# Second heads' keys and values three ticks later, a wider spread of the last convolution taps, and closer LayerNorm steps in a hybrid transformer block

## The chip, the core and the metric

The program runs on one core of one Trainium2 chip. The metric is the device time of one execution in microseconds (us), the median over several executions. The core has five engines that matter here, each of which works through its own instructions strictly in program order: PE (TensorE, matmuls and transposes; its weight loads are shown as PEld), DVE (VectorE), ACT (ScalarE), POOL (GpSimd) and SP, which here does nothing but issue DMAs. Engines meet through semaphores only.

## The reference, cut to what matters

One decoder layer on 512 tokens of width 2048, all in float32:

```python
h = rms_norm(x); proj = h @ w_in
out_a = dilated_mixture(aq, ak, av)          # 8 heads x 64, three (window, dilation) pairs
out_b = silu(layer_norm(causal_depthwise_conv31(bu * sigmoid(bg)) + conv_b))   # 512 channels
out_c = band_attention(cq, ck, cv, 127, sinks)   # 16 query heads, 2 key/value heads x 64
x = x + concat(out_a, out_b, out_c) @ w_out
h2 = rms_norm(x)
x = x + (silu(h2 @ w_gate) * (h2 @ w_up)) @ w_down    # width 5632
```

Queries and keys of both attentions are RMS-normalised per head first.

## The kernel before

Activations lie transposed, channels on the 128 partitions and the 512 tokens along the free axis. Each float32 factor is split in two parts of a reduced float type: a "high" part, cast by ACT, and a "low" part, the rest, subtracted by DVE (for the `mix` rows of attention C by POOL). A product is then three matmuls of 128x512: high x high, high x low and low x high (`mm3`, lines 325 to 327).

**The stages.** (1) The input projection, 30 column tiles of 128 (`PROJ`): four at once at the start, then 26 by `project`. (2) The output projection: 16 row tiles of `mix` (`ROWS`: c0 c3 c1 c5 c2 c7 c4 c6, then a0 a1 b2 b1 b0 b3 a2 a3) times 16 output tiles, in two halves: `half == 0` uses the eight c rows, `half == 1` the eight a and b rows. (3) The feed-forward part, with a seven-product scheme for its matrix products. It takes the last two thirds of the time and is not touched.

**The order of the work** is written by hand. `Ticks` is a list of functions with due times. The matmul loops call `ticks.tick()` at fixed places, and a tick emits everything that is due into the queues of the engines, in the order in which it was registered:

- `project` ticks once for two k steps, that is, every 6 matmuls, 8 ticks for a tile. The 26 tiles take ticks 0 to 207, so that tile number p of `PROJ` (from 0) is done at tick 8 x (p - 3).
- `first_two` (two output tiles together, 6 matmuls for each row) ticks after every row: 208 to 215 in half 0.
- The other 14 output tiles of half 0 tick after every 12 matmuls, twice for a tile: 216 to 243. Then comes half 1.

So attention heads, convolution and LayerNorm of earlier tiles run on DVE, ACT and POOL beside the projection matmuls, with their own few PE instructions (score matmuls, transposes, `weigh`) put between them.

**What touches the change.**

- Keys: `do_k` normalises a key tile (two heads), `twin` copies each head's half to the other half of the partitions with two DMAs on SP, `high` (L708 to L711) casts both heads on ACT and one tick later `low` (L713 to L715) subtracts both on DVE. Values of attention A: `load_v` fetches a tile from DRAM, `high` (L730 to L733) casts both heads and `low` (L735 to L737) subtracts them. Head 1 of a tile of A starts its scores 7 ticks after head 0 (`A_TICKS`), head 1 of C 12 ticks after head 0.
- Convolution: 4 channel tiles x 31 taps, each one DVE instruction (`tap`, L541), spread over the ticks. With n the tap's number, tap n >= 93 (the fourth tile) comes at tick 154, 156, 158, 160, 162, 163 and so on to 203, then a pause of 9 ticks, then 214, 216 and 217.
- LayerNorm over the 512 channels: `ln_sum` (three adds on DVE, then the split of the sum), `ln_mean` (a memset on DVE and two matmuls), `ln_center` (four DVE subtractions), `ln_square` (four squares on ACT, three adds on DVE), `ln_var` (`token_scale`: four PE transposes, a DVE reduction, a DVE scale and a power on POOL), `ln_out` (`all_rows`: a transpose on PE, a copy on ACT, a DMA to DRAM, `put`, and a DMA back that spreads the row over the partitions, `back`), `ln_scale` (four POOL products and four silu on ACT), and then `split_mix` of the rows b2, b1, b0, b3. They are at ticks 219, 221, 222, 225, 228, 231, 232 (put), 233 (back), 235 (scale) and 236 to 239 (splits).
- In `first_two` and after it, `split_rows(k)` emits the split of row k + 2 when row k is about to be multiplied. The low part of a c row is `ml_c`, on POOL (L1067).
- `residual` (L1168) adds an output tile to x on DVE. From the third output tile on, the accumulators are in two PSUM banks by turns (`column`), so a tile can begin when the add of the tile before the last is done.
- `next_unit` splits the weights two uses ahead (L283 on ACT, L284 on DVE) and issues weight loads (L271) on SP as buffers come free.

Of the kernel before, what the change touches and what calls it, by code (L numbers as in the profile page):

```python
# [9 lines left out]
F32 = mybir.dt.float32  # L10
F32R = mybir.dt.float32r
# [4 lines left out]
P = 128  # L16
T = 512
NT = T // P
# [10 lines left out]
TAPS = 31  # L29
NB = 4  # L30

OUT_ORDER = (list(range(16)), [n + o for n in range(6) for o in (0, 8)] + [6, 7, 14, 15])
TAPS_FROM, TAPS_FAST, TAP_TICKS = 19, 47, 1.8
TAPS_2 = 6
V_AHEAD = 2
WARM = 8
PAUSE_FROM, TAP_PAUSE = 205, 9


SQ, KW, VD, TD, EV = 3, 4, 4, 2, 1  # L40
# [2 lines left out]
ROW_KEYS = ("ck", "ak2")  # L43
FOLD_AT = (2, 4, 3)
FOLDED = 2 + sum(FOLD_AT) + 2
ROWS_FROM, ROWS_AT, LN_ROWS_AT = 2, (1, 2, 3), (1, 1, 2)


C_TICKS = (1, 6, 2, 2, 2, 2, 4, 1, 5)
# [86 lines left out]
def kernel(ctx: ExitStack, tc: tile.TileContext, xT, wi, wo, wgu, wd, cst_in, outT):  # L136
    nc = tc.nc
# [18 lines left out]
    ticks = Ticks()  # L156

    def slot(name, dt=F32, cols=T):
        return sp.tile([P, cols], dt, name=name, tag="s")
# [4 lines left out]
    def bank(name, cols=T):  # L164
        return psum["banks"].tile([P, cols], F32, name=name, tag="b")

    def column(name):
        return psum["tiles"].tile([P, T], F32, name=name, tag="c")
# [287 lines left out]
    for k in range(KT):  # L456
# [11 lines left out]
        hi, lo = h_hl.pop(k)  # L468
        h_hi.append(hi)
        h_lo.append(lo)  # L470
        for i in range(NT):
            s = slice(i * P, (i + 1) * P)
# [11 lines left out]
    def project(name):  # L484
        b = column(name)
        for half in range(2):
            wh, wl = next_unit(split=split_in_steps)
            for kk in range(8):
                k = 8 * half + kk
                s = slice(kk * P, (kk + 1) * P)  # L490
                mm3(b, wh[:, s], wl[:, s], h_hi[k], h_lo[k], k == 0, k == KT - 1)
                if kk % 2 == 1:
                    ticks.tick()
        return b

    def all_rows(out, src, heads, name, waits, then, *args):

        n = NT * heads
        b = bank(name + "t")
        nc.tensor.transpose(b[:n, :P], src, ident)  # L500
        rows = cp.tile([2 * NT, P], F32, name=name + "w", tag="rows", bufs=2)
        nc.scalar.copy(rows[:n], b[:n, :P])
        d = tc.dram_tile([n, P], F32, name=name)

        def put():
            nc.sync.dma_start(d, rows[:n])
            ticks.after(waits[1], back)

        def back():
            for h in range(heads):  # L510
                part = out if heads == 1 else out[HALF[h]]
                nc.sync.dma_start(part.rearrange("p (i c) -> p i c", i=NT),
                                  bass.AP(tensor=d.tensor, offset=d.offset + h * P,
                                          ap=[[0, P // heads], [heads * P, NT], [1, P]]))
            ticks.after(waits[2], then, *args)
        ticks.after(waits[0], put)
# [5 lines left out]
    hconv, yconv = {}, {}  # L522
# [22 lines left out]

    ln = {}

    def ln_sum():
        s = slot("lns")
        nc.vector.tensor_add(s, yconv[0], yconv[1])  # L550
        nc.vector.tensor_add(s, s, yconv[2])
        nc.vector.tensor_add(s, s, yconv[3])
        ln["hi"], ln["lo"] = slot("lnh", F32R), slot("lnl", F32R)
        nc.scalar.copy(ln["hi"], s)
        nc.vector.tensor_sub(ln["lo"], s, ln["hi"].bitcast(F32))
# [112 lines left out]
    def do_k(box, b, name, gi):  # L668
        def then(r):
            if name in ROW_KEYS:  # L670
                ticks.after(ROWS_FROM, rows_of, r)
            else:
                ticks.after(KW, widen, r)

        raw, at_r = head_scales(b, name, name == "ak2", then)
        box["k at"] = at_r + (ROWS_FROM + sum(ROWS_AT) - 2 if name in ROW_KEYS else KW) + TD + 7
        both = []

        def rows_of(r):
            wide = slot(name + "wide")  # L680
            all_rows(wide, r.rearrange("p a b -> p (a b)"), 2, name + "d", ROWS_AT, scale, wide)

        def widen(r):
            wide = slot(name + "wide")
            nc.scalar.copy(wide.rearrange("p (a b c) -> p a b c", a=NT, b=2),
                           r[:, :, :, None].to_broadcast([P, NT, 2, HD]))
            ticks.after(1, flip, wide)

        def flip(wide):
            b2 = bank(name + "t")  # L690
            for i in range(NT):
                nc.tensor.transpose(b2[:, i * P:(i + 1) * P], wide[:, i * P:(i + 1) * P], ident)
            ticks.after(1, scale, b2)

        def scale(b2):
            for h in range(2):
                both.append(slot(f"{name}{h}"))
                nc.vector.scalar_tensor_tensor(both[h][HALF[h]], raw[HALF[h]], gqk[HALF[h], gi:gi + 1], b2[HALF[h]],
                                               op0=ALU.mult, op1=ALU.mult)
            ticks.after(1, twin)  # L700

        def twin():
            for h in range(2):
                nc.sync.dma_start(both[h][HALF[1 - h]], both[h][HALF[h]])
            ticks.after(TD, high)

        def high():
            box["k"] = [(slot(f"{name}h{h}", F32R), slot(f"{name}l{h}", F32R)) for h in range(2)]  # L708
            for h in range(2):
                nc.scalar.copy(box["k"][h][0], both[h])  # L710
            ticks.after(1, low)  # L711

        def low():  # L713
            for h, (hi, lo) in enumerate(box["k"]):
                nc.vector.tensor_sub(lo, both[h], hi.bitcast(F32))  # L715
            if gi == 1:
                box["k0"] = [slot(f"{name}0{h}", F32R, 2 * P) for h in range(2)]
                for k0, src in zip(box["k0"], both):
                    nc.scalar.copy(k0[:, :P], src[:, :P])
                    nc.vector.tensor_sub(k0[:, P:], src[:, :P], k0[:, :P].bitcast(F32))  # L720

    def load_v(box, j):
        name = f"av{j}"
        t = slot(name + "s")
        nc.sync.dma_start(t.rearrange("p (i c) -> p i c", i=NT),
                          bass.AP(tensor=vd.tensor, offset=vd.offset + j * P, ap=[[T, P], [P * T, NT], [1, P]]))
        src = t.rearrange("p (a b c) -> p a b c", a=NT, b=2)

        def high():
            box["v"] = [slot(f"{name}{h}", F32R).rearrange("p (a b c) -> p a b c", a=NT, b=2) for h in range(2)]  # L730
            for h in range(2):
                nc.scalar.copy(box["v"][h][:, :, h], src[:, :, h])
            ticks.after(1, low)  # L733

        def low():  # L735
            for h, v in enumerate(box["v"]):
                nc.vector.tensor_sub(v[:, :, 1 - h], src[:, :, h], v[:, :, h].bitcast(F32))  # L737

        box["v at"] = ticks.now + V_AHEAD + 2
        ticks.after(V_AHEAD, high)  # L740

    def do_v(box, b, name):
        vs = slot(name + "s")
# [315 lines left out]
    mix, late = {}, []  # L1059
# [20 lines left out]
    g4 = b = None  # L1080
    taps = [(j, i) for j in range(NB) for i in range(TAPS)]
    for n, (j, i) in enumerate(taps):
        at_tap = TAPS_FROM + min(n, TAPS_FAST) + int(max(n - TAPS_FAST, 0) * TAP_TICKS) + TAPS_2 * (j >= 2)
        at_tap += TAP_PAUSE * (at_tap >= PAUSE_FROM)
        ticks.after(at_tap, tap, j, i)
    t_ln = at_tap + 2
    ticks.after(t_ln, ln_sum)
    ticks.after(t_ln + 2, ln_mean)
    ticks.after(t_ln + 3, ln_center)
    ticks.after(t_ln + 6, ln_square)  # L1090
    ticks.after(t_ln + 9, ln_var)
    ticks.after(t_ln + 12, ln_out, mix)

    shared = {}
    boxes, waiting = {}, []
    for name in PROJ[HEAD4:]:
        kind, what, j = name[0], name[1], name[2:]
# [3 lines left out]
        b = project(name)  # L1101
# [3 lines left out]
        if kind == "c":  # L1105
            box = Heads(shared) if j else shared
        else:
            box = boxes.setdefault(j, {})
# [15 lines left out]
    b = box = boxes = shared = waiting = None  # L1124
# [123 lines left out]
    for half in range(2):  # L1248
        for i, n in enumerate(OUT_ORDER[half]):
# [4 lines left out]
            if half == 1 and i == 2:  # L1254
                split_up_to(at["use"] + 1)
                ticks.drain()
                b = None
                open_banks(banks=4 - COLUMN_BANKS, high=2)
            b = column(f"o{half}_{n}")
            wh, wl = next_unit()  # L1260
            for kk in range(8):
                k = 8 * half + kk
# [4 lines left out]
                s = slice(kk * P, (kk + 1) * P)  # L1267
# [387 lines left out]
    for g in range(G_STEPS + N_DOWN):  # L1655
# [6 lines left out]
        for i, q in enumerate(ORDER):  # L1662
# [37 lines left out]
            n = LOADS + (t >= -2)  # L1700
# [3 lines left out]
            if N_TURNED - 2 <= t < N_TURNED:  # L1704
                n = 4 - (t % 2 == 0)
# [91 lines left out]
```

## Time and profile before

| what | us |
|---|---|
| median of 3 runs (lowest, highest) | 1850.84 (1850.51, 1851.1) |
| the profiled execution | 1851.08 |
| its span, first to last instruction | 1849.3 |
| PE busy in the span | 1841.7 |
| DVE, ACT, POOL busy | 1528.4, 1368.8, 1098.3 |

The profiled execution lies 0.24 us above the median and 1.8 us above its own span. Times of the trace are us from the start of the span. An instruction is shown with its line, engine, operation and tile names (output<-inputs, buffer numbers left out); a bracket at its end gives the idle time of its engine just before it and what released it. PE's matmuls overlap, so that their starts, not their durations, tell the pace.

### The profile page before, as it was taken

Reading aid. Unit: us, or ns where it says so; the run is one execution under the profiler, and the core shown is the slowest. Engines: PE = TensorE matmul, PEld = TensorE weight load, DVE = VectorE, ACT = ScalarE, POOL = GpSimd, SP = SyncE. Lnnn points to the kernel's source line nnn. Section 1 sums busy time; section 2 is a strip of 40 time slices with the busy share of each in tenths; the row PEclk is TensorE's granted clock in tenths of the full one; section 3 lists DMA queues with packets and bytes.
Section 4 is the critical chain, followed back from the end, with each engine's and each line's share of the span. In section 5 each row is a group of like instructions: output and inputs, shape, how many; then the busy total and the mean of one; then the engine's idle time right before and its main releaser. Section 6 shows DMA issues by size and latency. Waiting matters only on the chain.

```text
span 1849.3 us, 26795 instructions
## 1 busy us (share of the span) xinstructions
PE 1841.7 (100%) x8509; PEld 1533.7 (83%) x8509; DVE 1528.4 (83%) x2314; ACT 1368.8 (74%) x1957; POOL 1098.3 (59%) x703
## 2 busy tenths in 40 slices
PE   9999999999999999999999999999999999999999
PEld 7888888888888888888888888888888888888888
DVE  7688799997589888898888888888888677779887
ACT  6225655554466788889989889898898987777775
POOL 5004454462252568666685666857667777766786
PEclk9999999999999999999999999999999999999999
DMA  7435343433287359788787887787879786488984
GB/s 263 136 112 168 114 149 97 114 122 128 99 295 273 126 180 293 220 261 277 230 276 229 279 266 228 264 245 264 278 240 380 222 298 222 164 284 281 302 238 125
DMA packets 326461, 404.29 MB, mean 219 GB/s; under 512 B 81816, under 2 KB 216624, under 8 KB 326320
## 3 DMA queue, kind: packets, MB, share of 16 engines
q1 hardware_dynamic: 326176, 402.57, 67.8%
q8 instruction: 68, 1.11, 0.3%
q14 instruction: 73, 0.60, 0.1%
q10 hardware_dynamic: 144, 0.01, 0.0%
HBM read 312.31 MB, written 82.59 MB: 214 GB/s over the span
## 4 chain that ended last, share of the span: by engine, by line
PE 74%; DVE 0%; issue 0%; DVEq 0%
PE out L1446 62%; PE out L1338 6%; PE o L325 2%; PE o L326 2%; PE o L327 2%; PE out L1330 0%; PE a3o L935 0%; PE a3o L934 0%; PE a3t L910 0%; PE n2s L367 0%; DVE y L1635 0%; DVEq L1635 0%
## 5 line engine op out<-in xcount | busy, mean ns | idle before, releaser
L1446 PE MATMUL out<-wh,h 128*128 128x512 f32 x2464 | 609.0, 389 | 0.1
L1446 PEld LDWEIGHTS out<-wh,h 128*128 128x128 f32 x2464 | 462.3, 188 | 96.8 <-issue 0.5
L1446 PE MATMUL out<-wl,h 128*128 128x512 f32 x1232 | 329.3, 389 | 0.0
L1446 PEld LDWEIGHTS out<-wl,h 128*128 128x128 f32 x1232 | 231.2, 188 | 48.0
L1446 PE MATMUL out<-wh,a 128*128 128x512 f32 x896 | 221.3, 389 | 0.0
L1446 PEld LDWEIGHTS out<-wh,a 128*128 128x128 f32 x896 | 168.2, 188 | 34.9
L1446 PE MATMUL out<-wl,a 128*128 128x512 f32 x448 | 119.7, 389 | 0.0
L1549 DVE TENSOR_TENSOR G<-G,out 128x512 f32<-128x512 f32 x132 | 83.9, 677 | 18.1 <-PE out L1446 18.1
L1446 PEld LDWEIGHTS out<-wl,a 128*128 128x128 f32 x448 | 84.1, 188 | 17.5
L541 DVE SCALAR_TENSOR_TENSOR y<-bu,cst,y 128x511 f32<-128x511 f32 (+14 forms) x120 | 91.1, 759 | 1.5
L283 ACT CAST wh<-w 128x1024 fp32r<-128x1024 f32 (+1 forms) x41 | 42.0, 1030 | 53.4 <-PE o L326 27.9
L1338 PE MATMUL out<-a,wh 128*128 128x512 f32 x330 | 80.1, 391 | 0.0
L303 ACT CAST wh<-w 128x1024 fp32r<-128x1024 f32 x52 | 54.6, 1050 | 33.4 <-PE bg L326 8.7
L307 DVE TENSOR_TENSOR wl<-w,wh 128x1024 fp32r<-128x1024 f32 x52 | 66.4, 1279 | 9.5 <-ACT wh L303 9.4
L1546 DVE TENSOR_TENSOR G<-G,out 128x512 f32<-128x512 f32 x110 | 68.6, 681 | 5.7 <-PE out L1446 5.7
L1338 PEld LDWEIGHTS out<-a,wh 128*128 128x128 f32 x330 | 60.2, 188 | 11.4
L1587 DVE STREAM_TRANSPOSE z<-s 128x256 f32<-128x256 f32 x88 | 60.1, 683 | 3.0
L284 DVE TENSOR_TENSOR wl<-w,wh 128x1024 fp32r<-128x1024 f32 (+1 forms) x41 | 51.7, 1262 | 8.4 <-ACT wh L283 8.0
L325 PE MATMUL o<-mh_c,wh 128*128 128x512 f32 x128 | 51.4, 401 | 1.1 <-ACT a31e L866 1.1
L327 PE MATMUL o<-mh_c,wl 128*128 128x512 f32 x128 | 50.1, 391 | 0.0
L326 PE MATMUL o<-ml_c,wh 128*128 128x512 f32 x128 | 50.1, 391 | 0.0
L1491 DVE TENSOR_TENSOR Y<-Y,out 128x512 f32<-128x512 f32 x48 | 30.8, 685 | 17.9 <-PE out L1446 17.9
(2777 smaller groups left out, 5127.0 us busy)
## 6 DMA issues: line engine op xcount, KB each, us to landing
h<-hd SPq DMA_DIRECT2D x200, 256.0 KB, 5.7
od<-a SPq DMA_DIRECT2D x154, 256.0 KB, 6.6
a<-od SPq DMA_DIRECT2D x154, 256.0 KB, 5.9
w<-in_wi SPq DMA_DIRECT2D x59, 512.0 KB, 3.6
w<-in_wo SPq DMA_DIRECT2D x32, 512.0 KB, 3.4
hd<-h SPq DMA_DIRECT2D x56, 256.0 KB, 5.5
zd<-z SPq DMA_DIRECT2D x44, 256.0 KB, 4.8
x<-in_xT SPq DMA_DIRECT2D x16, 256.0 KB, 7.0
```

The lines of the kernel that those rows point to most:

```text
L284: eng.tensor_sub(lo[:, :n], t[:, :n], hi[:, :n].bitcast(F32))
L303: nc.scalar.copy(hi, t)
L307: nc.vector.tensor_sub(lo, t, hi.bitcast(F32))
L325: nc.tensor.matmul(out, wh, xh, start=start, stop=False)
L326: nc.tensor.matmul(out, wh, xl, start=False, stop=False)
L327: nc.tensor.matmul(out, wl, xh, start=False, stop=stop)
L541: nc.vector.scalar_tensor_tensor(yconv[j][:, i:], hconv[j][:, :T - i], c, yconv[j][:, i:], op0=ALU.mult, op1=ALU.add)
L1338: nc.tensor.matmul(out, lhs[:, s], rhs, start=begin, stop=last and low == flip[0] and x is xs[-1], skip_group_check=True)
L1446: nc.tensor.matmul(to[h], x[:, h * P:(h + 1) * P], v[:, j], start=sub == 0 and h not in started, stop=sub == 1 and n in (len(todo) - 1, le ...
L1546: op(t, t, b)
L1549: nc.vector.tensor_add(t, t, b)
L1587: nc.vector.transpose(to[:, :, h], s[:, cols].rearrange("p (c b) -> p b c", b=8))
```

## The change

It has three parts.

1. Keys' and values' head 1: `high` and `low` become functions of one head. Head 0 stays where it was, head 1 comes `OTHER` = 3 ticks later, for `do_k` and for `load_v`. The copies for the first key block of attention C (`k0`) go with their head.
2. Taps: taps of the fourth tile are 2.0 ticks apart (1.8 before), and the pause from tick 205 on is 5 ticks (9 before). They come at 154, 156 and so on by twos to 204, then at 211, 213, 215, 217 and 219.
3. LayerNorm: the first two adds of the sum move from DVE to POOL and to tick 209 (`ln_sum_3`); the rest comes at 221 (sum), 222 (mean), 223 (center), 224 (square), 226 (variance), 228 (out), 229 (put), 230 (back), 231 (scale), 232 to 235 (splits).

```diff
-TAPS_FROM, TAPS_FAST, TAP_TICKS = 19, 47, 1.8
+TAPS_FROM, TAPS_FAST, TAP_TICKS, TAP_TICKS_3 = 19, 47, 1.8, 2.0
-PAUSE_FROM, TAP_PAUSE = 205, 9
+PAUSE_FROM, TAP_PAUSE = 205, 5
+OTHER = 3
-ROWS_FROM, ROWS_AT, LN_ROWS_AT = 2, (1, 2, 3), (1, 1, 2)
+ROWS_FROM, ROWS_AT, LN_ROWS_AT = 2, (1, 2, 3), (1, 1, 1)
+LN_SUM_3, LN_AT = 12, (1, 2, 3, 5, 7)
...
+    def ln_sum_3():
+        s = ln["sum"] = slot("lns")
+        nc.gpsimd.tensor_add(s, yconv[0], yconv[1])
+        nc.gpsimd.tensor_add(s, s, yconv[2])
     def ln_sum():
-        s = slot("lns")
-        nc.vector.tensor_add(s, yconv[0], yconv[1])
-        nc.vector.tensor_add(s, s, yconv[2])
+        s = ln.pop("sum")
         nc.vector.tensor_add(s, s, yconv[3])
...
-            ticks.after(TD, high)
+                ticks.after(TD + h * OTHER, high, h)
+        def high(h):
+            hi, lo = box["k"][h] = (slot(f"{name}h{h}", F32R), slot(f"{name}l{h}", F32R))
+            nc.scalar.copy(hi, both[h])
+            ticks.after(1, low, h, hi, lo)
+        def low(h, hi, lo):
+            nc.vector.tensor_sub(lo, both[h], hi.bitcast(F32))
...
-        ticks.after(V_AHEAD, high)
+        for h in range(2):
+            ticks.after(V_AHEAD + h * OTHER, high, h)
...
-        at_tap = TAPS_FROM + min(n, TAPS_FAST) + int(max(n - TAPS_FAST, 0) * TAP_TICKS) + TAPS_2 * (j >= 2)
+        slow = max(n - 3 * TAPS, 0)
+        at_tap = TAPS_FROM + min(n, TAPS_FAST) + TAPS_2 * (j >= 2)
+        at_tap += int(max(n - slow - TAPS_FAST, 0) * TAP_TICKS + slow * TAP_TICKS_3)
         at_tap += TAP_PAUSE * (at_tap >= PAUSE_FROM)
     t_ln = at_tap + 2
+    ticks.after(t_ln - LN_SUM_3, ln_sum_3)
     ticks.after(t_ln, ln_sum)
-    ticks.after(t_ln + 2, ln_mean)
-    ticks.after(t_ln + 3, ln_center)
-    ticks.after(t_ln + 6, ln_square)
-    ticks.after(t_ln + 9, ln_var)
-    ticks.after(t_ln + 12, ln_out, mix)
+    for n, fn in enumerate((ln_mean, ln_center, ln_square, ln_var)):
+        ticks.after(t_ln + LN_AT[n], fn)
+    ticks.after(t_ln + LN_AT[4], ln_out, mix)
```

More of the change, by code (lines that the diff above doesn't have):

```diff
@@ L704, in twin @@
                 nc.sync.dma_start(both[h][HALF[1 - h]], both[h][HALF[h]])
-            ticks.after(TD, high)
-        def high():
-            box["k"] = [(slot(f"{name}h{h}", F32R), slot(f"{name}l{h}", F32R)) for h in range(2)]
+            box["k"] = [None, None]
             for h in range(2):
[L710 to L715, printed above, removed]
+                ticks.after(TD + h * OTHER, high, h)
[5 more added lines that the diff above has]
+            nc.vector.tensor_sub(lo, both[h], hi.bitcast(F32))
             if gi == 1:
[L717 to L720, printed above, removed]
+                k0 = slot(f"{name}0{h}", F32R, 2 * P)
+                box.setdefault("k0", []).append(k0)
+                nc.scalar.copy(k0[:, :P], both[h][:, :P])
+                nc.vector.tensor_sub(k0[:, P:], both[h][:, :P], k0[:, :P].bitcast(F32))
     def load_v(box, j):
@@ L727, in load_v, with high, low @@
         src = t.rearrange("p (a b c) -> p a b c", a=NT, b=2)
[L729 to L737, printed above, removed]
+        def high(h):
+            box["v"][h] = slot(f"{name}{h}", F32R).rearrange("p (a b c) -> p a b c", a=NT, b=2)
+            nc.scalar.copy(box["v"][h][:, :, h], src[:, :, h])
+            ticks.after(1, low, h)
+        def low(h):
+            v = box["v"][h]
+            nc.vector.tensor_sub(v[:, :, 1 - h], src[:, :, h], v[:, :, h].bitcast(F32))
+        box["v"] = [None, None]
         box["v at"] = ticks.now + V_AHEAD + 2
-        ticks.after(V_AHEAD, high)
+        for h in range(2):
+            ticks.after(V_AHEAD + h * OTHER, high, h)
     def do_v(box, b, name):
```

## Prediction

> **What bounds the kernel now.** I read the page first for the engine that is full, then whom PE waited for, then the queues at those places.
>
> ```profile
> span 1849.3 us, 26795 instructions
> ...
> PE 1841.7 (100%) x8509; PEld 1533.7 (83%) x8509; DVE 1528.4 (83%) x2314; ACT 1368.8 (74%) x1957; POOL 1098.3 (59%) x703
> ```
>
> PE is busy for 1841.7 of 1849.3 us. The change adds and removes no PE instruction: it can win only what PE loses between its instructions, or make PE lose more. The view of PE's waits lists the losses (us in total, times, longest):
>
> ```profile
> PE idle L416 <- DVE bones L356: 1.4, 1, 1.4
> PE o L325 <- ACT a31e L866: 1.1, 1, 1.1
> PE a0o L935 <- DVE a0pl L921: 0.7, 1, 0.7
> PE c60s L821 <- ACT c40e L866: 0.6, 1, 0.6
> PE lnm L562 <- DVE a21e L873: 0.3, 1, 0.3
> ```
>
> The first is the start of the program; the other four lie in stages that the change touches. Here they are in PE's timeline (start, duration, instruction, idle before it), with a fifth place at 394 us where PE is slowed without a gap that counts as idle:
>
> ```profile
> 280.09 0.27 PE L991 MATMUL c21t<-ident,c71e 128*128 128x128 f32 x1
> 280.93 0.38 PE L821 MATMUL c60s<-ck,cq 128*128 128x256 f32 x1 [0.57 <-ACT c40e L866]
> ...
> 366.19 0.33 PE L934 MATMUL a0o<-a0ph,av 128*128 128x256 f32 x1
> 367.22 0.39 PE L935 MATMUL a0o<-a0pl,av 128*128 128x256 f32 x1 [0.70 <-DVE a0pl L921]
> ...
> 394.36 0.48 PE L325 MATMUL o<-mh_c,wh 128*128 128x512 f32 x1
> 394.86 0.50 PE L326 MATMUL o<-ml_c,wh 128*128 128x512 f32 x1
> ...
> 421.64 0.39 PE L326 MATMUL o<-ml_c,wh 128*128 128x512 f32 x1
> 421.87 0.39 PE L327 MATMUL o<-mh_c,wl 128*128 128x512 f32 x1
> 422.53 0.47 PE L562 MATMUL lnm<-lnh,part 128*128 128x512 f32 x1 [0.28 <-DVE a21e L873]
> ...
> 481.20 0.39 PE L327 MATMUL o<-mh_c,wl 128*128 128x512 f32 x1
> 482.72 0.47 PE L325 MATMUL o<-mh_c,wh 128*128 128x512 f32 x1 [1.13 <-ACT a31e L866]
> ```
>
> A 128x512 matmul follows the one before after 0.23 (421.64 to 421.87); I take half of that, 0.11, for 256 columns and for a transpose (an estimate). The losses against that pace: 280.93 - 280.09 - 0.11 = 0.73; 367.22 - 366.19 - 0.11 = 0.92; 422.53 - 421.87 - 0.23 = 0.43; 482.72 - 481.20 - 0.23 = 1.29. Together 3.37. At 394 it is 394.86 - 394.36 - 0.23 = 0.27. These are all the change can win, 3.6 us or 0.2%.
>
> **The change part by part.** DVE's timeline at the first loss, at its last idle stretch before the second, and at the second, third and fourth:
>
> ```profile
> 276.37 2.09 DVE L715 TENSOR_TENSOR ak2l<-ak,ak2h 128x512 fp32r<-128x512 f32 x2
> 279.57 0.23 DVE L856 TENSOR_SCALAR c40d<-c40d,nsink 128x4 f32<-128x4 f32 x1
> ...
> 338.82 0.57 DVE L847 CUSTOM_DVE_ANT_0 a00s<-a00s,bias_a 128x384 f32<-128x384 f32 x1 [2.46 <-PE a00s L824]
> ...
> 365.87 0.76 DVE L737 TENSOR_TENSOR av<-av2s,av 128x256 fp32r<-128x256 f32 x2
> 366.74 0.42 DVE L921 TENSOR_TENSOR a0pl<-a0t,a0ph 128x256 fp32r<-128x256 f32 x1
> 367.08 0.72 DVE L541 SCALAR_TENSOR_TENSOR y<-bu,cst,y 128x489 f32<-128x489 f32 x1
> ...
> 416.63 0.98 DVE L551 TENSOR_TENSOR lns<-lns,y 128x512 f32<-128x512 f32 x1
> 422.22 0.17 DVE L560 MEMSET part<- 128x128 f32 x1
> ...
> 474.53 0.69 DVE L1067 TENSOR_TENSOR ml_b<-y,mh_b 128x512 fp32r<-128x512 f32 x1 [4.35 <-ACT mh_b L1066]
> 481.89 0.68 DVE L1168 TENSOR_TENSOR xr<-xr,o 128x512 f32<-128x512 f32 x1
> ```
>
> *Key halves, first loss.* ak2 is done at tick 120; its low parts come at tick 145, just ahead of c40's row maxima (tick 146), whose last step (279.57) releases c40's exponentials, and those free the score bank that c60s needs (tick 148). In the new order head 1's cast comes at 147, behind those exponentials, and its subtraction at 148. One of the two ak2l, 2.09 / 2 = 1.05, leaves the queue ahead of 279.57. That covers 0.73: gain 0.73. Late next would be c60's own maxima, with 1.05 more in front, at tick 152, four ticks of at least 1.4 each (6 x 0.23) after the subtraction; I cost that at nothing, covered by those 5.5 us; without the cover it costs 1.05.
>
> *Value halves and taps, second loss.* a0pl's last part is due at tick 195. The same tick has both av2 subtractions ahead of it; head 1's moves to 198: 0.38. ak1's head 1 moves from 192 to 195, still ahead, worth nothing. Between tick 178 and tick 195 the taps are 9 instead of 10 (0.72), and DVE has no idle stretch of over 0.1 there after the 2.46 that end at 338.82. 0.38 + 0.72 = 1.10 covers 0.92: gain 0.92. The wider taps themselves return 0.72 each at ticks 211 to 219, where there are five instead of three; DVE loses 1.44 there, but `ln_sum`'s two adds are gone from it. Casts, subtractions and slots are the same in number, and no DMA moves in the first two parts: `twin` and `load_v` issue as before.
>
> *The sum's first two adds, now on POOL.* They are emitted at tick 209, that is after row 1 of `first_two` and first in that tick, so behind row 3's low part and ahead of row 4's. POOL's timeline there, its group of six such low parts (busy us, mean ns | idle before them), one of them that ran long, and the four products of `ln_scale` (min/median/max ns):
>
> ```profile
> 390.47 1.29 POOL L1067 TENSOR_TENSOR ml_c<-mix_c,mh_c 128x512 fp32r<-128x512 f32 x1
> 391.75 1.75 POOL L877 TENSOR_SCALAR a11e<-a11e,a11d 128x384 f32<-128x384 f32 x1
> 393.47 2.78 POOL L1067 TENSOR_TENSOR ml_c<-mix_c,mh_c 128x512 fp32r<-128x512 f32 x2
> 396.24 1.73 POOL L877 TENSOR_SCALAR a11e<-a11e,a11d 128x512 f32<-128x512 f32 x1
> ...
> L1067 POOL TENSOR_TENSOR ml_c<-mix_c,mh_c 128x512 fp32r<-128x512 f32 x6 | 8.9, 1489 | 0.0
> ...
> 383.97 2.26 POOL L1067 TENSOR_TENSOR ml_c<-mix_c,mh_c 128x512 fp32r<-128x512 f32 x1
> ...
> L583 POOL TENSOR_TENSOR y<-y,lrs x4: 1284/1286/1298, 467.4 to 471.1; 128x512 f32<-128x512 f32 x4
> ```
>
> Each row starts as the one before ends, and the six ml_c from 382 to 401 us had no idle time before them (0.0, the last column of their group). Row 4's low part, the first of the two at 393.47, is what the matmul at 394.86 is short of: 393.47 + 1.39 (half of 2.78) = 394.86. So what is put ahead of it goes onto PE whole. The nearest rows are other two-input 128x512 operations of POOL: 1.28 (L583), 1.49 as the mean of the six from 382 to 401 us, 2.26 at most. I take the mean of that stretch: 2 x 1.49 = 2.98 lost, between 2.57 and 4.52, and nothing if the queue has run ahead by then. Rows 5 to 7 ask for no more: PE is late by the same amount, and POOL gives one low part after the other at its pace of before.
>
> *LayerNorm, third loss.* lnm waits for the memset at 422.22, which stands in DVE's queue behind everything up to tick 220. In the new order the two adds (the second took 0.98) are gone from this queue and lnm comes at 222, in the middle of an output tile, instead of 221, at a tile's end where a `residual` add and a weight subtraction stand ahead: gain 0.43. The closer steps: center (223) needs lnm; square (224) and variance (226) are two ticks apart, at least 2 x 12 x 0.23 = 5.5, in which DVE has three adds and about 3 us of other steps; variance to out (228) has again 5.5. I cost these at nothing; the cover is two ticks of matmuls for each.
>
> *LayerNorm, fourth loss.* ACT, SP and PE here:
>
> ```profile
> 468.68 0.81 ACT L585 ACTIVATE y<-y,cst 128x512 f32<-128x512 f32 x1 [3.39 <-POOL y L583]
> ...
> 451.85 0.33 SPq L271 DMA_DIRECT2D w<-in_wo  x1
> 460.25 0.32 SPq L506 DMA_DIRECT2D lrd<-lrdw  x1
> 463.31 0.35 SPq L512 DMA_DIRECT2D lrs<-lrd  x1
> ...
> 469.65 0.48 PE L325 MATMUL o<-mh_c,wh 128*128 128x512 f32 x1
> ```
>
> The view blames the exponential a31e. By the code the tile that begins at 482.72 needs the bank of the tile before the last, whose `residual` add on DVE ran from 481.89 to 482.57; DVE had sat 4.35 until 474.53 for ACT's mh_b, and ACT stood behind the silu, which waited for POOL, that is, for the broadcast (3.39 at 468.68). Everything from out on comes 3 to 4 ticks earlier, some 10 us, so that this jam is past when the tile of 482.72 begins: gain 1.29. What is late next: the silu's products start at tick 231. `put` stands in SP's queue ahead of the weight load of 451.85, `back` behind it; with 4.1 from the issue to POOL's start (463.31 to 467.4), the row would be there at about 452.7 + 4.1 = 456.8, the silu end near 463, the weight cast at 464, the weight subtraction at 465, the `residual` add for the tile that begins at tick 235 (469.65 in PE's row) at about 469. It fits by half a us: nothing, with 0 to 4 as its bounds.
>
> **The sum.** -0.73 - 0.92 - 0.43 - 1.29 + 2.98 = -0.39 us. On the profiled 1851.08 that is 1850.69, and on the median, 0.24 lower, 1850.45.
>
> **The rivals.** *POOL hides the adds.* For it: the DVE steps that feed POOL come earlier. Against: the group's idle time of 0.0. Then 3.37 is won: 1847.5.
>
> *The adds are slow.* POOL's rows of one shape take 1.28 or 2.26; if both adds fall on the long one, 4.52 - 3.37 = +1.15: 1852.0. The Trainium skill, page "SBUF — State Buffer", section "Who interferes with whom", says that a VectorE instruction with two SBUF inputs and a GpSimd instruction that reads SBUF exclude each other, the later one waiting for the whole of the earlier. By that rule, with DVE full here, this rival is the case. The trace agrees in part: 2.26 occurs once among six.
>
> *The moved halves free nothing.* If DVE's queue is as long at 279 and 366 us as before, only 0.43 + 1.29 is won: -1.72 + 2.98 = +1.26, 1852.1.
>
> *Slower: the jam moves instead of going.* If `back` lands late, ACT waits inside the silu, and with it the weight cast, the subtraction, the `residual` add and PE. Its place is tick 235. Beyond the half us of margin each us of delay is one of PE. It makes the change slower from 0.9 us of delay on (0.5 + 0.39); with 4 more, 1850.45 + 3.5 = 1854.0. Speaking for it: SP's queue is held by weight loads that wait for DVE. Against: `put` now stands ahead of one such load.
>
> **How the numbers follow.** My sum 0.50; POOL hides 0.20; slow adds 0.12; halves free nothing 0.10; the jam moves 0.08. The time is that of the likeliest, 1850.4 (1850.45). The range goes from the hidden adds, 1847.5, to the halves and slow adds with half the jam's price, 1853.0. The resolution of this kernel's measurement, 0.2%, is 3.7 us: faster than 1847.1 needs all of 3.64 and more, 0.04; slower than 1854.5 needs the jam with over 4 us, 0.05; the same 0.91. The sum's own range (2.57 to 4.52 for the adds, others as taken) is 1850.0 to 1852.0.
>
> **What would show it.** Right: no PE wait left at c60s, a0o, lnm and the tile of tick 239; a new wait of PE or PEld for ml_c at the fifth row of `first_two`, about 3 us, with two L552-like adds on POOL just before; PE's first-to-last time otherwise equal. Wrong: an ml_c wait under 1 us (adds hidden), a wait at the LayerNorm transposes (steps too close), or one at tick 235 (jam moved).

## The result and the profile after

| | median us (runs) | lowest to highest | profiled execution, its span |
|---|---|---|---|
| before | 1850.89 (22) | 1850.43 to 1853.45 | 1851.08, 1849.3 |
| changed | 1853.76 (22) | 1852.67 to 1855.0 | 1855.0, 1853.2 |

The ratio changed to before is 1.0014, with a 95% interval of 1.0007 to 1.002: the change costs 2.87 us where I had forecast a gain of 0.39. The interval lies above 1, so the change does cost time, though the 0.14% are less than the 0.2% that I had taken as what can be told. The profiled execution is the longest of the 22, 1.24 above the median; why comes out below.

The page and the view of PE's waits of the changed kernel (us in total, times, longest):

```profile
span 1853.2 us, 26799 instructions
...
PE 1843.6 (99%) x8509; PEld 1535.7 (83%) x8509; DVE 1529.4 (83%) x2312; ACT 1369.4 (74%) x1957; POOL 1102.4 (59%) x705
```

```profile
PE o L328 <- POOL ml_c L1073: 4.0, 2, 3.4
PE idle L418 <- DVE bones L358: 1.4, 1, 1.4
PE in L328 <- DVE wl L286: 0.4, 1, 0.4
PE c40t L997 <- POOL c60e L990: 0.3, 1, 0.3
```

All four lines that the change was to win (a0o, c60s, lnm, and the `residual` tile named under a31e) are gone, and one for ml_c has come. (The line for `in` stands in the program's first 20 us, ahead of all that was changed.) PE's timeline at these places, in order of time (lines are shifted: L997 was L991, L328 was L326, and so on):

```profile
280.00 0.27 PE L997 MATMUL c21t<-ident,c71e 128*128 128x128 f32 x1
280.03 0.36 PE L827 MATMUL c60s<-ck,cq 128*128 128x256 f32 x1
...
300.34 0.27 PE L997 MATMUL c40t<-ident,c40e 128*128 128x128 f32 x1
300.95 0.33 PE L997 MATMUL c40t<-ident,c60e 128*128 128x128 f32 x1 [0.34 <-POOL c60e L990]
...
365.79 0.33 PE L940 MATMUL a0o<-a0ph,av 128*128 128x256 f32 x1
365.96 0.28 PE L941 MATMUL a0o<-a0pl,av 128*128 128x256 f32 x1
...
390.49 0.39 PE L327 MATMUL o<-mh_c,wh 128*128 128x512 f32 x1
391.39 0.50 PE L328 MATMUL o<-ml_c,wh 128*128 128x512 f32 x1 [0.52 <-POOL ml_c L1073]
...
393.80 0.48 PE L327 MATMUL o<-mh_c,wh 128*128 128x512 f32 x1
397.71 0.80 PE L328 MATMUL o<-ml_c,wh 128*128 128x512 f32 x1 [3.44 <-POOL ml_c L1073]
398.31 0.63 PE L329 MATMUL o<-mh_c,wl 128*128 128x512 f32 x1
398.73 0.63 PE L327 MATMUL o<-mh_c,wh 128*128 128x512 f32 x1
...
486.42 0.39 PE L329 MATMUL o<-mh_c,wl 128*128 128x512 f32 x1
486.65 0.39 PE L327 MATMUL o<-mh_c,wh 128*128 128x512 f32 x1
```

c60s follows the transpose at once, a0o's second product comes after 0.17, the tile of tick 239 after 0.23: these gains are real. lnm's loss is gone too, but after PE had lost some 7 us at row 4; with the adds out of the way (e2 below) 0.31 of its 0.43 is still there. Three places are new. At c40t PE loses 300.95 - 300.34 - 0.11 = 0.50. At row 3 of `first_two` it loses 391.39 - 390.49 - 0.23 = 0.67. At row 4, which was short by 0.27 before, it loses 397.71 - 393.80 - 0.23 = 3.68. And behind row 4 the matmuls come every 0.43 instead of every 0.23. A table of windows around it (us, busy time and count of PE, PEld, DVE, ACT, POOL; granted clock, DMA share, GB/s) says why:

```profile
390.00:397.70 7.70, 3.76 (x20) 2.70 (x18) 7.59 (x15) 5.13 (x12) 7.62 (x7) 0.96 0.43 119
397.70:403.70 6.00, 5.99 (x14) 4.78 (x15) 5.90 (x9) 0.00 (x0) 5.22 (x4) 0.50 0.48 131
403.70:420.00 16.30, 16.30 (x82) 13.74 (x82) 15.17 (x36) 7.36 (x11) 6.30 (x5) 0.99 0.38 118
```

After the wait the granted clock is 0.50 for 6 us; half of those, about 3 us, are lost. PE counts as busy throughout, so the page's 99% does not show it: only the spacing of the starts and the clock column do.

In the profiled execution, then: 3.37 won; lost 0.50 (c40t), 0.67 (row 3), 3.68 - 0.27 = 3.41 (row 4) and about 3.0 (clock). That makes +4.2; the difference of the two executions is 3.92.

POOL at these places:

```profile
381.69 1.57 POOL L883 TENSOR_SCALAR a10e<-a10e,a10d 128x512 f32<-128x512 f32 x1 [1.56 <-DVE a10d L881]
...
390.05 1.28 POOL L1073 TENSOR_TENSOR ml_c<-mix_c,mh_c 128x512 fp32r<-128x512 f32 x1
391.29 1.81 POOL L552 TENSOR_TENSOR lns<-y,y 128x512 f32<-128x512 f32 x1
393.19 1.58 POOL L553 TENSOR_TENSOR lns<-lns,y 128x512 f32<-128x512 f32 x1
394.74 1.69 POOL L883 TENSOR_SCALAR a11e<-a11e,a11d 128x384 f32<-128x384 f32 x1
396.40 2.50 POOL L1073 TENSOR_TENSOR ml_c<-mix_c,mh_c 128x512 fp32r<-128x512 f32 x2
```

The adds stand where the prediction put them and hold the queue from 391.29 to 394.74, for 3.45. Row 4's low part ends at 396.40 + 1.25 = 397.65, and PE goes on at 397.71.

### The profile page after: what moved, and what is told of

The parts are those of the page before. It is cut to its first block, busy times and chain, and to the rows that moved or that the text cites. A ratio compares the mean times of both kernels' runs of the same rounds, so it can differ in the third digit from the quotient of the medians.

```text
span 1853.2 us, 26799 instructions
## 1 busy us (share of the span) xinstructions
PE 1843.6 (99%) x8509; PEld 1535.7 (83%) x8509; DVE 1529.4 (83%) x2312; ACT 1369.4 (74%) x1957; POOL 1102.4 (59%) x705
## 4 chain that ended last, share of the span: by engine, by line
PE 81%; DVE 2%; POOL 1%; issue 1%; ACT 0%; DMA 0%; SPq 0%; DVEq 0%; POOLq 0%; ACTq 0%
PE out L1453 62%; PE out L1345 6%; PE o L328 3%; PE o L329 3%; PE o L327 3%; PE aq L327 1%; PE aq L329 1%; PE aq L328 1%; DVE y L543 0%; POOL ml_c L1073 0%; DVE wl L309 0%; PE ak L327 0%; PE ak L329 0%; PE ak L328 0%; DMA w<-in_wi 0%
## 5 line engine op out<-in xcount | busy, mean ns | idle before, releaser
L328 PE MATMUL o<-ml_c,wh 128*128 128x512 f32 x128 | 51.2, 400 | 4.0 <-POOL ml_c L1073 4.0
```

The costliest lines, as they stand in the source:

```text
L328: nc.tensor.matmul(out, wh, xl, start=False, stop=False)
```

## The experiments

Every kernel was timed in five rounds beside the kernel before; ratios are to before, with their 95% intervals. "Undo" is an edit of the changed kernel, "alone" one of the kernel before.

An interval of 0.0009 to either side is 1.7 us. Only the larger steps below are clear by their intervals; the smaller ones rest on traces, one execution of each kernel, and on the spread of the runs: every run of e2 (highest 1850.11) and of e18 (1850.22) is below every run of before in the same rounds (lowest 1850.22 and 1850.29).

**Theory:** the gains are real, and the loss is the two adds in front of row 4, with the clock behind them. **Rivals:** the halves, the taps or the closer steps cost time themselves.

### The adds undone, moved, alone

e1_sum_on_dve leaves all adds on DVE, at tick 221:

```diff
-        nc.gpsimd.tensor_add(s, yconv[0], yconv[1])
-        nc.gpsimd.tensor_add(s, s, yconv[2])
+        nc.vector.tensor_add(s, yconv[0], yconv[1])
+        nc.vector.tensor_add(s, s, yconv[2])
...
-    ticks.after(t_ln - LN_SUM_3, ln_sum_3)
+    ticks.after(t_ln, ln_sum_3)
```

> The changed kernel with the first two adds of the LayerNorm sum back on DVE, at the tick of the sum (221); all else of the change stays. Theory A (the two POOL adds at tick 209 hold up row 4's low part, PE stands over 3 us, and then its clock is granted at half for some 6 us): no ml_c wait over 0.7 us, granted clock 1.000, time 1850.9 - 3.4 = 1847.5. Theory B (the moved halves or the taps now at 211 to 219 crowd POOL there by themselves): the ml_c wait stays at 2 us or more and the time at 1852 to 1854.

Measured: 1850.8 against 1851.06, 0.9996 (0.9988 to 1.0005). Row 4 is short by 0.36 and the clock stays at 1.00. But the view of waits has a new line:

```profile
PE lnm L567 <- DVE part L565: 1.3, 1, 1.3
```

With three adds in DVE's queue the mean, one tick behind the sum, is too early: PE loses 1.48 at lnm, standing for DVE. The wait at row 4 and the slow clock went as expected; the time did not come down to the 1847.5 that I had expected.

e2_pool_adds_217 keeps the adds on POOL, eight ticks later, when `first_two` has all its rows:

```diff
-LN_SUM_3, LN_AT = 12, (1, 2, 3, 5, 7)
+LN_SUM_3, LN_AT = 4, (1, 2, 3, 5, 7)
```

> The changed kernel with the two POOL adds at tick 217 instead of 209, where POOL's queue has gaps. Theory A: no ml_c wait over 0.7 us, clock 1.000, 1847.5, as with the adds on DVE or a few tenths better. Theory B: still 1852 to 1854.

Measured: 1849.75, 0.9991 (0.9982 to 1.0). No wait at row 4 beyond 0.36, clock 1.00. So this place, and not the adds as such, is what costs. The time misses 1847.5 again. What is left in this trace: c40t 0.46, row 3 0.69, row 5 0.22, lnm 0.31, together 1.68 of the 3.37.

e3_pool_adds_alone puts only the two adds on POOL, at tick 209, into the kernel before (`ln_sum_3` as in the change):

```diff
+    ticks.after(t_ln - 10, ln_sum_3)
```

> The kernel before with one edit: the first two adds of the sum on POOL at tick 209; halves, taps and the other LayerNorm steps as before. Theory A: an ml_c wait of 3 us or more at row 4, then matmuls at a pace of 0.43 instead of 0.23 us; 1854 to 1857 (3 us of wait alone, 7 with the slow clock, less 0.4 at lnm). Theory B: within 1 us of before, since the crowding comes from the other parts.

Measured: 1854.75, 1.0017 (1.0008 to 1.0027), +3.69 from this part alone. Here POOL took almost exactly what the prediction had assumed, 391.49 to 394.53:

```profile
391.49 1.30 POOL L550 TENSOR_TENSOR lns<-y,y 128x512 f32<-128x512 f32 x1
392.87 1.67 POOL L551 TENSOR_TENSOR lns<-lns,y 128x512 f32<-128x512 f32 x1
394.53 1.68 POOL L880 TENSOR_SCALAR a11e<-a11e,a11d 128x384 f32<-128x384 f32 x1
```

PE loses 2.72 at row 4 (0.27 before), and seven matmuls then come at 0.43.

### The other parts alone

e5_halves_alone, e6_taps_alone and e7_steps_alone each put one part into the kernel before. e5 is part 1 of the change for keys and values, in short:

```diff
+OTHER = 3
...
-            ticks.after(TD, high)
+                ticks.after(TD + h * OTHER, high, h)
...
-        ticks.after(V_AHEAD, high)
+            ticks.after(V_AHEAD + h * OTHER, high, h)
```

e6 is these constants and the line that uses them; the sum and all behind it come two ticks later with the last tap:

```diff
-TAPS_FROM, TAPS_FAST, TAP_TICKS = 19, 47, 1.8
+TAPS_FROM, TAPS_FAST, TAP_TICKS, TAP_TICKS_3 = 19, 47, 1.8, 2.0
-PAUSE_FROM, TAP_PAUSE = 205, 9
+PAUSE_FROM, TAP_PAUSE = 205, 5
```

e7 is the closer steps of part 3 in full, with POOL's two adds four ticks ahead of the sum, clear of row 4:

```diff
+LN_SUM_3, LN_AT = 4, (1, 2, 3, 5, 7)
...
+    ticks.after(t_ln - LN_SUM_3, ln_sum_3)
```

> The kernel before with the first part alone: head 1's keys and values three ticks later. Theory A (each part wins what its PE wait was worth, but PE then meets POOL's queue at row 3 of first_two): the c60s wait gone (-0.73), the a0o wait shorter by 0.38 or gone, a new ml_c wait at row 3 of 0.3 to 0.7: 1850.0 to 1850.5. Rival (POOL comes earlier by as much as PE): no ml_c wait at row 3, 1849.8. Rival (the halves are worth nothing): 1850.9.

> The kernel before with the second part alone: the fourth tile's taps 2.0 apart and a pause of 5; the LayerNorm steps keep their old distances and so come 2 ticks later. Theory A: the a0o wait shorter by 0.7 (one tap fewer ahead of it), the c60s wait as before, and the silu jam 2 ticks nearer to half 1, so that the wait at the tile of tick 239 stays 1.3 or moves: 1850.2 to 1851.5. Rival (taps are worth nothing): 1850.9 with a0o as before.

> The kernel before with the third part alone, its two POOL adds 4 ticks ahead of the sum (tick 215, where POOL has gaps) instead of at tick 209. Theory A: the waits at lnm and at the tile of tick 239 go (-0.43 and -1.29), c60s and a0o stay: 1849.2. Rival (the closer steps put new waits at their transposes, or the jam moves to tick 235): 1850.5 or more.

Measured: halves 1850.94 against 1851.16, 0.9998 (0.999 to 1.0007); taps 1852.11, 1.0005 (0.9996 to 1.0014); steps 1856.78, 1.0029 (1.0018 to 1.0041).

The halves do free c60s (0.73) and half of a0o (0.49 left), but the same trace has c40t 0.51 and row 3 0.37: nearly all is returned. The taps free a0o and return it at row 3 (0.53), row 5 (0.22), lnm (1.0 instead of 0.43) and the tile of tick 239 (1.47 instead of 1.29), and the median is above the 1850.2 to 1851.5 that I had expected. I had not expected the steps to cost 5.6 alone. Their trace, in the view of waits and in the timelines of POOL and DVE:

```profile
PE lnm L566 <- DVE part L564: 3.9, 1, 3.9
```

```profile
405.96 2.34 DVE L285 TENSOR_TENSOR wl<-w,wh 128x1024 fp32r<-128x1024 f32 x2
406.29 3.21 POOL L551 TENSOR_TENSOR lns<-y,y 128x512 f32<-128x512 f32 x1
408.23 1.79 DVE L542 SCALAR_TENSOR_TENSOR y<-bu,cst,y 128x483 f32<-128x483 f32 x1
409.58 1.60 POOL L552 TENSOR_TENSOR lns<-lns,y 128x512 f32<-128x512 f32 x1
...
423.18 0.17 DVE L564 MEMSET part<- 128x128 f32 x1
```

The mean's matmul comes 4 us before DVE reaches the memset that feeds it, and the clock falls behind that wait too (0.50 in the window 424.4 to 427.2); another 1.14 are lost at an output tile (416.58) whose `residual` add was late. The tile of tick 239 loses nothing, as expected. The mean one tick behind the sum is far too close here; with the other two parts around it the same step lost 0.31 (e2). The rows show a second price of an add on POOL: the tap beside it took 1.79 (0.71 five us later, at 413.53), and the add itself 3.21 (1.30 in e3). The Trainium skill, page "SBUF — State Buffer", section "Who interferes with whom", says that these two engines exclude each other here and that the later one waits for the whole of the earlier. The trace agrees as far as durations can tell: the add starts beside two weight subtractions of DVE, which end at 408.30 (405.96 + 2.34) and at 1.17 each are no longer than one without it (1.22 at 416.35), and it ends 1.20 after them, at 409.50; the tap, from 408.23, ends 0.52 behind the add.

e10_after_mean brings only the steps behind the mean closer, without touching sum and mean (`LN_ROWS_AT` as in the change):

```diff
-    ticks.after(t_ln + 6, ln_square)
-    ticks.after(t_ln + 9, ln_var)
-    ticks.after(t_ln + 12, ln_out, mix)
+    ticks.after(t_ln + 4, ln_square)
+    ticks.after(t_ln + 6, ln_var)
+    ticks.after(t_ln + 8, ln_out, mix)
```

> The kernel before with the LayerNorm steps closer only behind the mean: sum 219 and mean 221 as before, all adds on DVE; then center 222, square 223, variance 225, out 227, put 228, back 229, scale 230. Theory A (the wait at the tile of tick 239 came from the silu jam; earlier silu removes it, and the bad lnm wait of 4 us came from the mean one tick behind the sum): the tick 239 wait goes (-1.29), no new wait at the transposes, c60s and a0o as before: 1849.7. Rival (the jam only moves, to tick 231 to 235): 1850.5 or more with a wait there.

Measured: 1852.52 against 1851.01, 1.0011 (1.0003 to 1.002). 1849.7 had been expected. The wait at tick 239 is gone and another stands 18 us earlier: 464.20 - 461.81 - 0.23 = 2.16. Three of the 11 runs have a mean clock of 0.999.

```profile
461.81 0.39 PE L327 MATMUL o<-mh_c,wl 128*128 128x512 f32 x1
464.20 0.47 PE L325 MATMUL o<-mh_c,wh 128*128 128x512 f32 x1 [2.00 <-ACT mh_b L1066]
```

This is the rival "the jam moves", in the kernel before. In the changed kernel the same steps come one tick later (out at 228, here 227), and there no such wait occurs.

### How long a wait, and what the clock makes of it

e8_half_pool_add leaves half of one add on POOL at tick 209 (128x256; the rest on DVE at 221), e4_one_pool_add one whole add, e11_three_adds both and a third that nobody reads (its edit):

```diff
+        again = slot("again")
+        nc.gpsimd.tensor_add(again, yconv[0], yconv[1])
```

> The changed kernel with one of the two adds on POOL at tick 209; the second is on DVE at tick 221. Theory A with a clock that falls only after PE stood for more than about 3 us (3.4 in the changed kernel's profile, against 1.1 in the one before, after which the pace stayed): a wait near 2 us, pace 0.23 after it, 1847.5 + 1.8 + 0.4 = 1849.7. If the clock falls after any wait of 1.5 us or more: 1852.5.

> The changed kernel with half of one add on POOL at tick 209 (the first 256 columns); the other half and the second add are on DVE at tick 221. It asks from what length of wait the clock falls: one add made PE wait 2.75 us start to start and slowed the matmuls after it to 0.43, waits of 1.5 did not. Theory A (a fall only after some 2.5 us): a wait of 1.3 to 1.8 at row 4, pace 0.23 after it, no more than 1 us above the variant with the adds back on DVE (1850.8): 1851.0 to 1851.8. Rival (it falls after 1.5 too): matmuls at 0.43 and 1852.5.

> The changed kernel with one more add of 128x512 on POOL at tick 209 (its output is not used). Theory A (each add there is a wait of PE of its own duration, 1.6 to 1.8, and the slow clock costs up to 3 us once, whatever the length): the row 4 wait 5.3 start to start, matmuls at 0.43 for some 6 us after it, 1853.8 + 1.7 = 1855.5. Rival (the slow stretch grows with the wait): 1857 or more.

| kernel | row 4, start to start, in the trace | matmuls at 0.43 behind it | median, ratio | runs with mean clock below 1.0 |
|---|---|---|---|---|
| e8, half an add | 2.31 | 0 | 1851.29, 1.0001 (0.9992 to 1.001) | 4 of 11 |
| e4, one add | 2.75 | 7 | 1851.39, 1.0 (0.9991 to 1.0009) | 1 of 11 |
| e3, two adds alone | 2.95 | 7 | 1854.75, 1.0017 (1.0008 to 1.0027) | 11 of 11 |
| changed, two adds | 3.91 | 12 | 1853.76, 1.0014 (1.0007 to 1.002) | 19 of 22 |
| e11, three adds | 5.32 | 11 | 1855.82, 1.0026 (1.0016 to 1.0037) | 8 of 8 |

e4's timeline, where one sees the clock fall a us behind the wait and rise again 3 us later:

```profile
393.67 0.48 PE L327 MATMUL o<-mh_c,wh 128*128 128x512 f32 x1
396.42 0.49 PE L328 MATMUL o<-ml_c,wh 128*128 128x512 f32 x1 [2.27 <-POOL ml_c L1073]
...
397.45 0.58 PE L329 MATMUL o<-mh_c,wl 128*128 128x512 f32 x1
397.84 0.63 PE L327 MATMUL o<-mh_c,wh 128*128 128x512 f32 x1
...
400.40 0.63 PE L940 MATMUL a1o<-a1ph,av 128*128 128x512 f32 x1
400.82 0.44 PE L941 MATMUL a1o<-a1pl,av 128*128 128x512 f32 x1
```

So the clock's price does not grow with the wait from 3.9 to 5.3 (12 and 11 matmuls); it comes or does not come, by the run. The granted clock, taken in short windows, was at one half for 3.41 us in e3, e4 and e7 and for 6.83 in the changed kernel and e11 (in e4: 397.0 to 397.6 at 0.91, to 400.8 at 0.50, to 401.2 at 0.87, which makes 0.11 + 3.20 + 0.10). The short ones began 0.6 to 1.1 us after PE had resumed, the long ones 0.7 and 1.2 us before it did, and the length of the wait alone does not decide: e7's 3.90 has a short one, the changed kernel's 3.44 a long one. In the changed kernel the three runs with a mean clock of 1.0 took 1852.67, 1852.68 and 1852.77, the median 1853.76, the only one with 0.998, the profiled one, 1855.0. The clock is worth 1853.76 - 1852.68 = 1.08 in the median and 2.3 in the profiled execution, which is why that one lies so high. A mean clock of 0.999 fits a stretch of 3.4 us in 1853 (1 - 1.7 / 1853 = 0.9991), 0.998 one of 6.8; the last digit hides less than 1 us lost. The Trainium skill, page "TensorE: Matmul & The Clock Gate", section "Part 1: The HAM clock gate", says that activity is judged in windows of about 3.4 us that run freely, and that an idle one halves the clock. Free windows agree with a price that comes by the run, and slow stretches of 3.41 and 6.83 with one window and two; that the clock fell at a gap of 2.27, where no window of 3.4 can have been idle throughout, does not.

### Where the gains went

The gains were 3.37, and e2 keeps only 1.31. These runs ask what takes the rest.

e9_row3_early is e2 with row 3's split registered one tick earlier, and e12_mean_later is e1 with the mean and all behind it one tick later (`LN_AT` (2, 3, 4, 6, 8)).

> The variant with the POOL adds at tick 217, and the split of row 3 (c5) registered for tick 207 instead of at row 1 of first_two, so that its low part stands ahead of the head products of tick 207 in POOL's queue. Theory A (what PE wins upstream it gives back at row 3, because POOL's queue comes only some 0.7 us earlier where PE comes 1.4 earlier): the row 3 wait of 0.69 goes, the row 4 loss stays at 0.3 to 0.7, 1849.75 - 0.4 = 1849.3. Rival (the wait only moves to row 4, POOL's total being the floor): 1849.75, with row 4 losing 1.0.

> The changed kernel with all three adds on DVE at tick 221 and the mean and all that follows one tick later (223, 224, 225, 227, 229; scale 232). Theory A (with the adds on DVE it is the mean one tick behind the sum that cost 1.49 at lnm): that wait falls to 0.5 or less, the rest as in the variant with the adds on DVE (1850.8): 1849.7. Rival (DVE is behind at this place by its load, not by the distance): a wait of 1 or more stays, 1850.5.

Measured: e9 1849.41 against 1851.01, 0.999 (0.9982 to 0.9999); e12 1849.57, 0.9991 (0.9982 to 1.0). e9 missed its purpose: within the tick a11's products were registered earlier and stayed ahead of row 3 on POOL, so its order is e2's, and so is its row 3 (0.64): the 1849.3 that I had expected came about by luck. e12 shows that e1's 1.48 at lnm was the single tick between sum and mean: it is 0.39 now, with all adds on DVE.

The last four start from e12. e13_row3_206 splits row 3 at tick 206, which does put it ahead of two of a11's products. e14_rows_early splits the first five rows from tick 193 on; its edit:

```diff
-        if name == PROJ[-1]:
-            for n, row in enumerate(ROWS[:3]):
+        if name == PROJ[-2]:
+            for n, row in enumerate(ROWS[:5]):
```

e17_other1 sets `OTHER` to 1; e18_rows_other1 has both edits.

> Against e12 (1849.57 us): row 3 of first_two is split at tick 206, ahead of two of a11's products in POOL's queue. Theory 'POOL's queue is the floor': PE's wait at row 3 (0.68 in e12) goes and row 4's (0.35) grows to 0.7 to 1.0, as POOL ends the same work at the same time: 1849.3 to 1849.7. Rival 'row 3 waits for something else': row 3 stays at 0.68 and row 4 at 0.35, 1849.6.

> Against e12 (1849.57 us): the first five rows of first_two are split from tick 193 on, in POOL's idle time before 382 us. Theory 'POOL's queue is the floor': the waits at rows 3, 4 and 5 (0.68, 0.35, 0.20 in e12) all go and c40t's 0.54 and lnm's 0.40 stay: 1849.57 - 1.23 = 1848.3. Rival 'the gain returns again': a11's products, now later, hold PE at a11 or another place and the time is 1849.3 or more.

> Against e12 (1849.57 us): the second head comes one tick later, not three. Theory 'c40t's 0.54 comes from the sigmoid's table load, which stands behind the wait for DVE': the load is free of the wait again, c40t's wait goes, and with it 0.54, of which row 3, POOL's floor, takes back up to 0.54 (it would then be 1.2): 1849.0 to 1849.6. Rival: the cast one tick after head 0's stands ahead of c40's exponentials, and c60s's 0.6 to 0.7 is back: 1849.6 with waits at both c60s and row 3.

> Against e14: the second head one tick later, as in e17, with the first five rows split early. Theory (table load and POOL's floor, both): the waits at c40t and at rows 3 to 5 are gone, 1849.57 - 0.54 - 1.23 = 1847.8, the sum of the four gains of before less lnm's 0.40. Rival: one of the waits is handed on to a11 or to lnm, 1848.5 or more.

| kernel | median against 1850.82 | ratio | PE's losses left (us) |
|---|---|---|---|
| e13 | 1849.7 | 0.9994 (0.9985 to 1.0002) | c40t 0.47, ak3t 0.46, lnm 0.55 |
| e14 | 1849.61 | 0.9992 (0.9983 to 1.0001) | c40t 0.48, a0o 1.09 and 0.85 |
| e17 | 1849.51 | 0.9991 (0.9982 to 1.0) | rows 3 to 5: 0.71, 0.36, 0.22; lnm 0.86 |
| e18 | 1848.4 | 0.9987 (0.9978 to 0.9996) | a0o 0.28 and 0.65, lnm 0.44 |

*Row 3.* In e12 PE lost c40t 0.48, row 3 0.68, row 4 0.35, row 5 0.21 and lnm 0.39. e13 removes row 3's loss, and about as much stands at ak3t and lnm; row 4, which by the theory of POOL's floor was to grow to 0.7 to 1.0, fell to 0.20. e14 removes those of rows 3 to 5 and returns them at a0o, where DVE is late: its weight subtraction, beside a split that POOL now does at that place, takes 2.30 (1.21 in e12), and it then waits 0.59 for ACT, which had such a row's cast in its queue (mh_c).

POOL's, DVE's and PE's timelines of e14 there:

```profile
360.50 1.64 POOL L1073 TENSOR_TENSOR ml_c<-mix_c,mh_c 128x512 fp32r<-128x512 f32 x1
...
360.92 2.30 DVE L309 TENSOR_TENSOR wl<-w,wh 128x1024 fp32r<-128x1024 f32 x1
...
365.54 0.33 PE L940 MATMUL a0o<-a0ph,av 128*128 128x256 f32 x1
366.74 0.39 PE L941 MATMUL a0o<-a0pl,av 128*128 128x256 f32 x1 [0.87 <-DVE a0pl L927]
```

So row 3 waits for POOL's order, as supposed, but what is taken off it comes back through DVE: e14 gained nothing, where 1848.3 had been expected.

*c40t.* ACT's timeline around the sigmoid, first of the kernel before, then of the changed one, then of e17:

```profile
284.04 1.28 ACT L531 ACT_TABLE_LOAD   x1
291.22 0.63 ACT L531 ACTIVATE bg<-bg 128x512 f32<-128x512 f32 x1 [5.89 <-DVE bg L530]
```

```profile
290.91 1.28 ACT L533 ACT_TABLE_LOAD   x1 [7.31 <-DVE bg L532]
292.20 0.63 ACT L533 ACTIVATE bg<-bg 128x512 f32<-128x512 f32 x1
...
L533 ACTq EVENT_SEMAPHORE  x1: 17/17/17, 290.9 to 290.9; - x1
```

```profile
291.01 0.63 ACT L533 ACTIVATE bg<-bg 128x512 f32<-128x512 f32 x1 [6.27 <-DVE bg L532]
```

Before, the table load ran inside ACT's wait for DVE. In the changed kernel the wait sits on the load, so that its 1.28 comes behind it, and c60's exponentials, POOL's product and c40t with them. With `OTHER` = 1 the wait is on the sigmoid again, and c40t's loss is gone. By itself that wins nothing (e17, 1849.51; e12 had 1849.57): lnm loses 0.86 for 0.39. Rows 3 to 5 lose what they lost in e12, though I had expected them to take the gain back: counted from the transpose ahead of c60s, PE reaches row 3 0.50 earlier, and its low part starts on POOL 0.46 earlier. With the early rows too the gain arrives (e18, 1848.4, the fastest of all these kernels, 2.42 below before; 1847.8 had been expected). The changed kernel has a semaphore instruction of 17 ns on the sigmoid's line, at 290.9 ahead of the load; e5, e12 and e13 have it too, and before, e6, e17 and e18, whose load is free, do not. So a wait has become an instruction of its own, ahead of the load. Why it did is open: a second thing to wait for, the cast moved to tick 147, is likely, as e5 (halves alone) shows the same and `OTHER` undoes it, but the two heads' parts were not tried one by one.

## Why the prediction was wrong

The sum was -0.39; +2.87 was measured. Its terms, from the medians:

| term | predicted | measured | from |
|---|---|---|---|
| gains of halves, taps, steps | -3.37 | -1.31 | e2, adds out of the way |
| the two adds at tick 209 | +2.98 | +3.10 | changed, runs at clock 1.0 (1852.68 - 1850.89 = 1.79), less e2's -1.31 |
| the clock behind that wait | not named | +1.08 | 1853.76 - 1852.68 |
| sum | -0.39 | +2.87 | |

The measured column adds up by construction, as its second term is a difference.

*The adds* were sized right: place, queue order, the row of `first_two`, and 3.10 for 2.98 (POOL's queue was held for 3.45 in the trace). "POOL hides the adds" was wrong at tick 209; it is right at tick 217 (e2).

*The step that failed most* is "Together 3.37 ... all the change can win", each gain then counted whole. Every wait named did vanish, but PE arriving earlier meets the next queue: 1.31 was won. I asked what is late next only at the place of each loss and cost it at nothing; it was late at other places, at c40t behind the table load (0.50) and at row 3 of `first_two` (0.67). Row 3 in the kernel before, with the DVE step that feeds POOL ahead of it, and that step in the changed kernel:

```profile
392.09 0.39 PE L326 MATMUL o<-ml_c,wh 128*128 128x512 f32 x1
...
382.17 0.16 DVE L875 RECIPROCAL a10d<-a10d 128x1 f32<-128x1 f32 x1
```

```profile
381.43 0.16 DVE L881 RECIPROCAL a10d<-a10d 128x1 f32<-128x1 f32 x1
```

Before, row 3's low part was done at 391.76 (390.47 + 1.29), 0.33 ahead of PE. In the changed kernel PE is ready for it at 390.72 (390.49 + 0.23), 1.37 earlier, but it starts on POOL only 0.42 earlier (390.05). POOL's work up to it starts with a10e, 0.26 after DVE's a10d in both kernels (at 382.43, where the view of before names PE as the releaser, and at 381.69), and a10d is only 0.74 earlier; so DVE's queue and POOL's together could not follow PE. The prediction had quoted the group of six ml_c with idle time 0.0 and used it for the loss alone; for the gains it never asked how much earlier POOL and DVE would be. Which of the two holds the other is not shown; neither is a fixed floor, as in e17 row 3's part came earlier with PE (0.46 and 0.50).

*The second failure* is the missing term. I put a 3 us wait on PE as 3 us and nothing behind it; the clock behind it cost 1.08 in the median. The kernel before ran at a clock of 1.00 with no wait of PE over 1.4, so its trace could not have shown this, and a bound for it was due.

*The halves free nothing* was wrong at its places (c60s and a0o went) and near right in its amount: e5 gains 0.2. *The adds are slow*, at 4.52 for the two, was too much at tick 209: 1.81 and 1.58 here and 1.30 and 1.67 in e3, nearer to my 2.98; at tick 215 it was the case (3.21 and 1.60 in e7). *The jam moves* did not happen in the changed kernel (no wait between 430 and 500 us) but does in e10. The range ended at 1853.0, named as the halves and slow adds with half the jam's price; but by the prediction's own terms the first two alone make 1850.84 - 1.72 + 4.52 = 1853.6, and half of the jam's 3.5 more 1855.4. The upper bound was added up wrongly, and no case had a clock.

*What the closer steps need* I costed at nothing with "two ticks of matmuls" as the cover. In the changed kernel the steps behind the mean had it; the mean one tick behind the sum did not (e7, e1), and moving it by one tick won 1.2 (e12 against e1).

## To carry over

A gain at one wait is worth only what the other queues can follow: sum gains stage by stage up to the next queue that will be late, not over the span. A stall of 2 us or so on the matmul engine (2.27 in e4) can cost its own length and then some us at half clock, so look at the spacing of starts behind it, not at busy time. When a step moves, look on which instruction its consumer's wait ends up; if that is a table load, the load is no longer hidden.

## What the runs showed of the hardware

- The granted clock fell to half after PE had waited 2.27 (e4) to 4.85 us (e11) and stayed there for 3.4 (e3, e4, e7) or 6.8 us (changed, e11); after 1.83 it did not in the trace of e8, though 4 of that kernel's 11 runs have a mean clock of 0.999. Between runs of the same kernel it comes and goes.
- One 128x512 add on POOL took 1.30 to 3.21 us, and a DVE instruction beside it up to 1.1 us more (1.79 for a tap of 0.71). An add moved to POOL is not free for DVE.
- A wait of an activation can stand ahead of its table load, as a semaphore instruction of its own: 1.28 us that were hidden before (284.04) came behind the wait (290.91).
